# The gate columns of the dense experts: two matmuls per token in the rounded 32-bit format in place of one fp32 matmul

## The chip, the cores and the metric

The kernel runs on one core of a Trainium2 chip. The metric is the device time of one execution in microseconds (us). Before the change three runs gave 3235.85, 3254.53 and 3223.81 us, a median of 3235.85 us.

## What is computed

One encoder layer over 1024 tokens of width 1024: gated attention and convolution, then a retrieval layer over 128 x 128 = 16384 small experts, then a norm. The change lies in the retrieval layer, which in the reference is:

```python
q = (xc @ w_query).reshape(c, PEER_HEADS, 2, PEER_HALF_DIM)
sc = jnp.einsum('chpd,hpnd->chpn', q, sub_keys)
s1, i1 = lax.top_k(sc[:, :, 0], PEER_TOPK)
s2, i2 = lax.top_k(sc[:, :, 1], PEER_TOPK)
cand = (s1[..., :, None] + s2[..., None, :])       # 16 x 16 sums per head
top, pos = lax.top_k(cand, PEER_TOPK)              # 16 experts per head, 8 heads
g = softmax(top)                                    # one gate per chosen expert
a = gelu(einsum('chkd,cd->chk', expert_u[eidx], xc))
out = einsum('chk,chkd->cd', g * a, expert_v[eidx])
```

Each token so has 128 chosen experts (8 heads of 16), each named by two key numbers from 0 to 127 and carrying one gate.

## The kernel before, in words

The tokens are cut into eight tiles of 128. The first five (640 tokens, group B) are served **densely**: every one of the 16384 experts is computed for them by matmul and multiplied by a gate that is zero where the expert was not chosen. The last three (384 tokens, group A) are served by **gathering** the chosen rows of the expert tables with indirect DMAs. Order of the work: queries, keys and values for all tokens; the mixer, output product and expert scores of group B; then the same for group A; then the expert stage, in which the dense products (`passes`, L905) and the gathered rows (`gather_gen`, L739 to L755) run side by side.

The change lies in `weights_gen` (L686). It makes the dense gates of group B while group A's mixer runs. For each of the five tiles, here called a chunk, it waits until the selection has filled `chosen`, transposes the two key numbers and the gate (`ptw`, L703), so that the 128 chosen experts of a token lie on the partitions, and copies the gates to `w` (tile `wtr`, L707). Then 32 steps follow, each for four tokens (`WQ`). In a step VectorE (DVE) compares the key numbers with a row of numbers, which gives the one-hot matrices `ms` (L714); GpSimd (POOL) multiplies the first with the gates, `o1` (L718); ScalarE (ACT) copies the second, `o2` (L720). Both write with another order of the two free dimensions than they read. One step later `finish` (L691) has TensorE (PE) multiply `o2` and `o1` for each of the four tokens (`pw`, L695): over the 128 chosen experts this sums the gates into a 128 x 128 table of key pairs. ACT copies the table to `wbuf` (L696), and after each 32 tokens `wbuf` is written to HBM (`w_d`, L726). The expert stage reads `w_d` back (`wt`, L920) and multiplies it with the experts' outputs (L930). In the profile the tiles `o1` and `o2` are both called `o`.

`ms`, `o1` and `o2` have two buffers each (`WFB = 2`), and so has the PSUM tile `pw`. A buffer of `o1` is free for a later step once PE has done the `pw` matmuls that read it; a buffer of `ms` is free once POOL and ACT have read it.

Elsewhere the kernel already uses the rounded 32-bit format (`F32R`): `put` (L183) writes a rounded copy of a tile on ACT and the rest, tile less copy, on DVE, and `gemm` (L220) and `passes` (L901) make three matmuls of such pairs: high by high, high by low, low by high.

The order of the work is set in two steps. Generators such as `weights_gen` and the selection are advanced by `tick`, which the large products call with an estimate of their time (a step of the gates each 1.6 us of it, `W_STEP`). What is written then goes through a scheduler, which settles the order on each engine's queue before the kernel runs; on the chip each engine works through its own queue in that order.

Of the group A work, `mix` (L524) computes the rows of the output product and their norm, in tiles of a ring called `mixw`, and `repeated_iota` (L111) makes the rows of numbers.

Of the kernel before, what the change touches and what calls it, by code (L numbers as in the profile page):

```python
# [10 lines left out]
F32 = mybir.dt.float32  # L11
BF16 = mybir.dt.bfloat16
F32R = mybir.dt.float32r
# [3 lines left out]
ALU = mybir.AluOpType  # L17
# [3 lines left out]
P = 128  # L21
# [14 lines left out]
NK = 128  # L36
# [15 lines left out]
WQ = 4  # L52
# [5 lines left out]
MIXW = 3  # L58
# [7 lines left out]
def block_kernel(ctx, tc, x, wqkv, wcols, wpr, wo, wq, skT, uv, uT, an_w, fn_w, fin_w, sub_w,  # L66
                 conv_w, lq1, lk1, lq2, lk2, cosT, sinT, out):
    nc = tc.nc
    V, A, PL, PE, SP = nc.vector, nc.scalar, nc.gpsimd, nc.tensor, nc.sync
# [4 lines left out]
    def pool(name, bufs=1, stack=None, **kw):  # L74
        return (stack or left).enter_context(tc.tile_pool(name=name, bufs=bufs, **kw))
# [30 lines left out]
    def rows_bcast(pl, src, n, name, tag=None, bufs=None):  # L106
        t = pl.tile([P, n], F32, name=name, tag=tag or name, bufs=bufs)
        SP.dma_start(out=t, in_=bass.AP(tensor=src.tensor, offset=src.offset, ap=[[0, P], [1, n]]))
        return t

    def repeated_iota(pl, dst, tag="iota"):  # L111
        n = dst.shape[1]
        row = pl.tile([P, n], F32, name="iota", tag=tag, bufs=2)
        PL.iota(row, pattern=[[1, n]], base=0, channel_multiplier=0, allow_small_or_imprecise_dtypes=True)
        V.tensor_copy(out=dst, in_=row.unsqueeze(2).broadcast_to(list(dst.shape)))

# [55 lines left out]
    def norm_rows(src, w_b, dst, junk, tag):  # L172
        ss = tiny.tile([P, 1], F32, name=f"ss_{tag}", tag=f"ss_{tag}")
        A.activation(junk, src, AF.Square, accum_out=ss)
        r = rstd_of(ss, D, 1, tag)
        V.scalar_tensor_tensor(dst, src, r, w_b, op0=ALU.mult, op1=ALU.mult)
# [22 lines left out]
    def transposes(src, dst, t0):  # L199
        for k0 in range(0, KD, 4):  # L200
            if isinstance(dst, tuple):
                to = lambda pt, k0=k0: put(dst, (slice(None), slice(k0, k0 + 4), slice(t0, t0 + P)), pt)
            else:
                to = dst[:, k0:k0 + 4, t0:t0 + P]
            four_transposes(to, [src[:, (k0 + k) * P:(k0 + k + 1) * P] for k in range(4)])
# [8 lines left out]
    def units_k(wp, src, n):  # L214
        u = [unit(wp, src[n, i], 512) for i in range(2)]
        return [tuple(t[:, k % 4, :] for t in u[k // 4]) for k in range(KD)]
# [3 lines left out]
    def gemm(pd, lhs, rhs, us=0.853):  # L220
        n = len(lhs)
        for i in range(n):
            l, r = lhs[i], rhs[i]
            if not isinstance(l, tuple):
                l, r = (l,), (r,)
            c = THREE if len(l) == 2 else ((0, 0),)
            for j, (a, b) in enumerate(c):
                PE.matmul(pd, lhsT=l[a], rhs=r[b], start=i == 0 and j == 0, stop=i == n - 1 and j == len(c) - 1)  # L228
        tick(us * n)

    def kts(op, sl):
        if isinstance(op, tuple):
            return [tuple(t[:, k, sl] for t in op) for k in range(op[0].shape[1])]
        return [op[:, k, sl] for k in range(op.shape[1])]

    def row(wk, name):
        return wk.tile([P, D], F32, name=name, tag="row")
# [286 lines left out]
    def mix(tt0, nt, c0, keep_hn, rings, mT, hnT, outer=None):  # L524
        with ExitStack() as st:
            if outer:
                st = outer
            wk = pool("mixw", nt + MIXW, stack=st)
            fn_b = rows_bcast(pool("mixn", stack=st), fn_w, D, "fn_b")
            xts = []  # L530
            for i in range(nt):
                tt = tt0 + i
                xts.append(row(wk, "xt2"))
                SP.dma_start(out=xts[i], in_=x[tt * P:(tt + 1) * P, :])
            later = []
            for j in range(2):
                w = units_k(rings[j], wo, j)
                for i in range(nt):
                    tt, xt = tt0 + i, xts[i]
                    ph = ps["g"].tile([P, 512], F32, name="ph2", tag="g")  # L540
                    gemm(ph, kts(mT, slice(c0 + i * P, c0 + (i + 1) * P)), w)
                    V.tensor_add(xt[:, j * 512:(j + 1) * 512], ph, xt[:, j * 512:(j + 1) * 512])
                    if j == 1:
                        SP.dma_start(out=h_d[tt * P:(tt + 1) * P, :], in_=xt)
                        hn = row(wk, "hn")
                        norm_rows(xt, fn_b, hn, hn, "h")
                        if keep_hn:
                            SP.dma_start(out=hn_d[tt * P:(tt + 1) * P, :], in_=hn)
                        if later:
                            transposes(*later.pop(0))  # L550
                        later.append((hn, hnT, c0 + i * P))
            if outer:
                return lambda: transposes(*later.pop(0))
            transposes(*later.pop(0))
# [131 lines left out]
    def weights_gen(wf):  # L686
        later = []
        iota_t = wf.tile([P, NK, WQ], BF16, name="iota_t", tag="iota_t", bufs=1)
        repeated_iota(wf, iota_t, "wtr")

        def finish(buf, q, o1, o2):  # L691
            for t in range(0, WQ, 4):
                pw = ps["w"].tile([P, 4, NK], F32, name="pw", tag="g")
                for u in range(4):
                    PE.matmul(pw[:, u, :], lhsT=o2[:, t + u, :], rhs=o1[:, t + u, :], start=True, stop=True)  # L695
                A.copy(out=buf[:, :, q + t:q + t + 4], in_=pw.rearrange("p t i -> p i t"))  # L696

        for c in range(NB):
            while c >= len(chosen):
                yield  # L700
            pt = ps["w"].tile([P, 4, P], F32, name="ptw", tag="g")
            for j, s in enumerate(chosen[c]):
                PE.transpose(out=pt[:, j, :], in_=s, identity=ident)  # L703
            ib = wf.tile([P, 2, P], BF16, name="ib", tag="ib", bufs=2)
            A.copy(out=ib, in_=pt[:, 0:2, :])
            w = wf.tile([P, P], F32, name="wtr", tag="wtr", bufs=2)
            A.copy(out=w, in_=pt[:, 2, :])  # L707
            for b in range(P // WT):
                buf = wf.tile([P, NK, WT], F32, name="wbuf", tag="wbuf", bufs=1)
                for q in range(0, WT, WQ):  # L710
                    ts = slice(b * WT + q, b * WT + q + WQ)
                    sh = [P, NK, WQ]
                    ms = wf.tile([P, 2] + sh[1:], BF16, name="ms", tag="ms")
                    V.tensor_tensor(out=ms, in0=ib[:, :, ts].unsqueeze(2).broadcast_to([P, 2] + sh[1:]),  # L714
                                    in1=iota_t.unsqueeze(1).broadcast_to([P, 2] + sh[1:]), op=ALU.is_equal)
                    o1 = wf.tile([P, WQ, NK], F32, name="o1", tag="o1")
                    o2 = wf.tile([P, WQ, NK], F32, name="o2", tag="o2")
                    PL.tensor_tensor(out=o1.rearrange("p t i -> p i t"), in0=ms[:, 0],  # L718
                                     in1=w[:, ts].unsqueeze(1).broadcast_to(sh), op=ALU.mult)
                    A.copy(out=o2.rearrange("p t i -> p i t"), in_=ms[:, 1])  # L720
                    if later:
                        finish(*later.pop(0))
                    later.append((buf, q, o1, o2))
                    yield
                finish(*later.pop(0))
                A.dma_start(out=w_d[c * (P // WT) + b], in_=buf)  # L726
# [131 lines left out]
    n = NA * P  # L858
# [9 lines left out]
    ms = pa.enter_context(ExitStack())  # L868
# [4 lines left out]
    ps["g"] = pspool("ps_x1", 4, pa)  # L873
    hnT = operand(pool("hnA", stack=pa), [P, KD, n], "hnT")
    mix(NB, NA, 0, True, (wring, wring), mT, hnT)
    with ExitStack() as st:
        sk = pool("sk1", stack=st).tile([P, 2 * PH, NK], F32, name="sk")
# [165 lines left out]
```

## Time and profile before

| what | value |
|---|---|
| median of three runs | 3235.85 us (3223.81 to 3254.53) |
| profiled execution | 3236.47 us |
| its span in the trace | 3234.7 us |
| PE matmul busy | 3017.4 us, 93% |
| PE weight load busy | 2768.1 us, 86% |
| DVE busy | 2647.0 us, 82% |
| ACT busy | 1298.3 us, 40% |
| POOL busy | 954.6 us, 30% |

The span is the time from the first to the last instruction in the trace; some 2 us lie around it. The busy times of PE and of its weight load overlap. Matmuls are pipelined, so the pace of a run of matmuls is read from the distance of their starts, not from the duration of one. A matmul on fp32 operands leaves two records of PE and two of its weight load; a matmul in the rounded format leaves one of each.

### The profile page before, as it was taken

How to read it: one execution, taken by the hardware profiler on the slowest of the kernel's cores; microseconds unless marked ns; L12 is line 12 of the kernel's file. 1: busy time of each engine (PE TensorE's matmuls, PEld its weight loads, DVE VectorE, ACT ScalarE, POOL GpSimd, SP SyncE). 2: the span in 40 equal slices, each digit the busy share in tenths (PEclk: the TensorE clock that was granted, in tenths of full speed). 3: DMA queues.
4: the chain of work that ended last, by engine and by line, in shares of the span. 5: the costliest groups of instructions: out<-in, count | busy, mean ns of one | idle time of the engine just before them, and what ended most of it. 6: DMA issues, size and time to landing. Idle time of an engine off the chain costs nothing.

```text
span 3234.7 us, 46047 instructions
## 1 busy us (share of the span) xinstructions
PE 3017.4 (93%) x17551; PEld 2768.1 (86%) x17551; DVE 2647.0 (82%) x4665; ACT 1298.3 (40%) x2344; POOL 954.6 (30%) x716
## 2 busy tenths in 40 slices
PE   7999999898999889799999999999999999999992
PEld 6799988798888779798989989889888999998891
DVE  4442565478999996798999999999999999998898
ACT  3322464335567757433333333333333333333332
POOL 2310000045444444232223323322333323233333
PEclk9999999999999989899999999999999999999996
DMA  5451232555444374787888888878789899988997
GB/s 177 146 177 66 82 111 92 211 164 202 146 177 182 148 269 161 265 297 274 304 291 293 308 286 315 323 275 316 268 301 339 325 348 338 339 329 317 327 331 288
DMA packets 237550, 801.12 MB, mean 248 GB/s; under 512 B 18832, under 2 KB 123280, under 8 KB 174096
## 3 DMA queue, kind: packets, MB, share of 16 engines
q0 software_dynamic: 64704, 442.53, 37.4%
q1 hardware_dynamic: 152592, 305.30, 27.2%
q10 hardware_dynamic: 20032, 50.34, 4.1%
q8 instruction: 138, 2.26, 0.3%
q14 instruction: 84, 0.69, 0.1%
HBM read 714.74 MB, written 83.36 MB: 247 GB/s over the span
## 4 chain that ended last, share of the span: by engine, by line
PE 36%; DVE 20%; issue 18%; DMA 15%; POOL 7%; ACT 3%; SPq 0%; POOLq 0%; ACTq 0%; DVEq 0%
DMA wt<-w_d 7%; PE z L905 7%; POOL uvt L739 6%; PE pg L228 4%; DMA uvt<-in_uv,idx 4%; PE pq L228 4%; PE pout L905 4%; DVE acc L755 3%; PE ph L228 3%; DVE uvt L746 3%; PE held L905 2%; PE py L228 2%; PE pw L695 2%; DVE hacc L957 2%; PE pv L228 1%
## 5 line engine op out<-in xcount | busy, mean ns | idle before, releaser
L739 POOL DMA_INDIRECT uvt<-in_uv,idx x384 | 552.6, 1439 | 1297.0 <-DVE acc L755 852.8
L905 PE MATMUL z<-actTh,uh 128*128 128x320 f32 x2048 | 636.7, 311 | 2.1 <-ACT pr L929 1.1
L905 PE MATMUL z<-actTh,uhl 128*128 128x320 f32 x2048 | 637.6, 311 | 0.0
L905 PE MATMUL z<-actTl,uh 128*128 128x320 f32 x2048 | 636.1, 311 | 0.0
L746 DVE SCALAR_TENSOR_TENSOR uvt<-uvt,hng 128x1024 f32<-128x1024 f32 x384 | 472.7, 1231 | 48.6 <-DMA uvt<-in_uv,idx 42.9
L755 DVE SCALAR_TENSOR_TENSOR acc<-uvt,wt,acc 128x1024 f32<-128x1024 f32 x381 | 486.4, 1277 | 6.1 <-ACT wt L749 4.8
L905 PEld LDWEIGHTS z<-actTh,uh 128*128 128x128 f32 x2048 | 387.1, 189 | 12.2 <-ACT pr L929 2.1
L905 PEld LDWEIGHTS z<-actTl,uh 128*128 128x128 f32 x2048 | 387.4, 189 | 8.8
L905 PEld LDWEIGHTS z<-actTh,uhl 128*128 128x128 f32 x2048 | 387.9, 189 | 4.0
L905 PE MATMUL pout<-vh,ph 128*128 128x512 f32 x768 | 306.5, 399 | 47.0 <-DVE hacc L957 30.2
L748 ACT ACTIVATE wt<-zt 128x1 f32<-128x1 f32 x384 | 77.5, 202 | 668.4 <-DVE uvt L746 667.5
L905 PE MATMUL pout<-vhl,ph 128*128 128x512 f32 x768 | 302.7, 394 | 0.0
L905 PE MATMUL pout<-vh,phl 128*128 128x512 f32 x768 | 301.9, 393 | 0.6 <-DVE phl L898 0.6
L718 POOL TENSOR_TENSOR o<-ms,wtr 128x512 f32<-128x512 bf16 x160 | 204.7, 1322 | 256.5 <-PE pw L695 127.3
L957 DVE TENSOR_TENSOR hacc<-pout,hacc 128x512 f32<-128x512 f32 x384 | 260.5, 681 | 2.8 <-PE pout L905 2.8
L185 DVE TENSOR_TENSOR wl<-wr,wh 128x2048 fp32r<-128x2048 f32 x66 | 157.2, 2382 | 118.8 <-ACT wh L184 114.7
L896 ACT CAST ph<-pr 128x640 fp32r<-128x640 f32 x128 | 93.3, 729 | 394.2 <-DVE pr L930 394.2
L905 PEld LDWEIGHTS pout<-vh,ph 128*128 128x128 f32 x768 | 145.7, 190 | 78.7 <-DVE hacc L957 39.5
L695 PE MATMUL pw<-o,o 128*128 128x128 f32 x1280 | 172.3, 288 | 39.8 <-POOL o L718 20.2
L184 ACT CAST wh<-wr 128x2048 fp32r<-128x2048 f32 x74 | 141.1, 1909 | 168.8 <-DMA wr<-in_wq 41.5
L695 PEld LDWEIGHTS pw<-o,o 128*128 128x128 f32 x1280 | 164.3, 201 | 47.7 <-POOL o L718 26.9
L905 PE MATMUL held<-vh,ph 128*128 128x512 f32 x512 | 200.6, 392 | 0.7 <-ACT ph L896 0.7
(290 smaller groups left out, 6760.4 us busy)
## 6 DMA issues: line engine op xcount, KB each, us to landing
raw<-in_uT SPq DMA_DIRECT2D x128, 512.0 KB, 6.5
raw<-in_uv SPq DMA_DIRECT2D x128, 512.0 KB, 8.0
w_d<-wbuf ACTq DMA_DIRECT2D x20, 2048.0 KB, 7.0
wt<-w_d SPq DMA_DIRECT2D x32, 1280.0 KB, 16.0
wr<-in_wcols SPq DMA_DIRECT2D x28, 1024.0 KB, 5.1
wr<-in_wq SPq DMA_DIRECT2D x24, 1024.0 KB, 5.2
xt<-in_x SPq DMA_DIRECT2D x16, 512.0 KB, 4.0
q_d<-qt POOLq DMA_DIRECT2D x32, 256.0 KB, 3.5
```

What stands on the lines that cost most here:

```text
L184: A.copy(out=op[0][sl], in_=src)
L185: lo.tensor_sub(op[1][sl], src, op[0][sl].bitcast(F32))
L228: PE.matmul(pd, lhsT=l[a], rhs=r[b], start=i == 0 and j == 0, stop=i == n - 1 and j == len(c) - 1)
L695: PE.matmul(pw[:, u, :], lhsT=o2[:, t + u, :], rhs=o1[:, t + u, :], start=True, stop=True)
L718: PL.tensor_tensor(out=o1.rearrange("p t i -> p i t"), in0=ms[:, 0], in1=w[:, ts].unsqueeze(1).broadcast_to(sh), op=ALU.mult)
L739: PL.indirect_dma_start(out=t[:], out_offset=None, in_=uv, in_offset=bass.IndirectOffsetOnAxis(ap=sels[c][1][:, k:k + 1], axis=0))
L746: V.scalar_tensor_tensor(u, u, 1.0, st[c], op0=ALU.mult, op1=ALU.mult, accum_out=zt)
L748: A.activation(wt, zt, AF.Gelu)
L755: V.scalar_tensor_tensor(st["acc"], v, wt, st["acc"], op0=ALU.mult, op1=ALU.add)
L896: A.copy(out=hi, in_=t)
L905: PE.matmul(ps, lhsT=lhs[k][a], rhs=rhs[k][b], start=first and k == 0 and j == 0, stop=last and k == n - 1 and j == 2)
L957: V.tensor_add(hacc[:, t - NR, ds], ps, hacc[:, t - NR, ds])
```

## The change

The table of a token is made by two matmuls in the rounded format in place of one in fp32. The gate is split in a rounded part (ACT) and a rest (DVE). POOL makes a one-hot matrix for each part, so `o1` doubles in size, and both are summed in PSUM. `o2` holds zeros and ones and is written once, in the rounded format. To make room, the row of numbers and `w` have one buffer in place of two, and `mix` of group A has five tiles in its ring in place of six.

```diff
-    def repeated_iota(pl, dst, tag="iota"):
+    def repeated_iota(pl, dst, tag="iota", bufs=2):
...
-            wk = pool("mixw", nt + MIXW, stack=st)
+            wk = pool("mixw", nt + MIXW - (tt0 > 0), stack=st)
...
-        repeated_iota(wf, iota_t, "wtr")
+        repeated_iota(wf, iota_t, "wtr", 1)
...
                 for u in range(4):
-                    PE.matmul(pw[:, u, :], lhsT=o2[:, t + u, :], rhs=o1[:, t + u, :], start=True, stop=True)
+                    for j in range(2):
+                        PE.matmul(pw[:, u, :], lhsT=o2[:, t + u, :], rhs=o1[:, j, t + u, :],
+                                  start=j == 0, stop=j == 1)
...
-            w = wf.tile([P, P], F32, name="wtr", tag="wtr", bufs=2)
-            A.copy(out=w, in_=pt[:, 2, :])
+            w = wf.tile([P, 2, P], F32R, name="wtr", tag="wtr", bufs=1)
+            A.copy(out=w[:, 0, :], in_=pt[:, 2, :])
+            V.tensor_sub(w[:, 1, :], pt[:, 2, :], w[:, 0, :].bitcast(F32))
...
-                    o1 = wf.tile([P, WQ, NK], F32, name="o1", tag="o1")
-                    o2 = wf.tile([P, WQ, NK], F32, name="o2", tag="o2")
-                    PL.tensor_tensor(out=o1.rearrange("p t i -> p i t"), in0=ms[:, 0],
-                                     in1=w[:, ts].unsqueeze(1).broadcast_to(sh), op=ALU.mult)
+                    o1 = wf.tile([P, 2, WQ, NK], F32R, name="o1", tag="o1")
+                    o2 = wf.tile([P, WQ, NK], F32R, name="o2", tag="o2")
+                    for j in range(2):
+                        PL.tensor_tensor(out=o1[:, j].rearrange("p t i -> p i t"), in0=ms[:, 0],
+                                         in1=w[:, j, ts].bitcast(F32).unsqueeze(1).broadcast_to(sh), op=ALU.mult)
```

## Rows read from the trace of the kernel before

**Rows 1.** Busy us by stretch: start:end, length, PE, PEld, DVE, ACT, POOL, clock, DMA, GB/s
```profile
727.00:858.00 131.00, 117.19 (x748) 115.09 (x747) 118.04 (x358) 77.25 (x101) 64.90 (x41) 0.96 0.49 179
858.00:974.00 116.00, 106.01 (x667) 102.54 (x666) 111.20 (x299) 75.35 (x104) 50.35 (x38) 0.96 0.47 173
974.00:1095.00 121.00, 110.96 (x750) 103.46 (x748) 118.55 (x292) 94.41 (x169) 51.68 (x43) 0.96 0.41 153
1095.00:1214.00 119.00, 96.09 (x568) 86.58 (x566) 111.69 (x273) 74.62 (x102) 55.04 (x42) 0.91 0.67 245
1214.00:1316.00 102.00, 99.58 (x692) 98.63 (x691) 67.27 (x154) 72.58 (x106) 43.29 (x34) 1.00 0.46 165
1316.00:3234.00 1918.00, 1806.58 (x9984) 1636.87 (x9982) 1753.69 (x2642) 632.96 (x1314) 585.59 (x402) 0.98 0.86 310
```

**Rows 2.** Instructions of line L707: ns min/median/max, first and last start, us
```profile
L707 ACT COPY wtr<-ptw x5: 271/280/286, 727.2 to 1214.8; 128x128 f32<-128x128 f32 x5
```

**Rows 3.** Chain of waits from 727 to 1316 us: share of the stretch by line
```profile
by line: PE pq L228 10.9%; PE pw L695 9.6%; issue 9.3%; DVE ms L714 7.5%; PE ph L228 4.7%; PE pg L228 4.4%; DVE wl L185 4.2%; ACT o L720 3.5%; DMA sc<-sc_d 3.3%; DVE tk L590 2.8%; DVE nm L387 2.1%; POOL o L718 1.9%; DVE si L592 1.8%; DMA w_
```

**Rows 4.** Chain of waits from 1200 to 1360 us: start, us, what
```profile
1241.27 1.78 PE pw L695 x16
...
1315.83 10.15 DMA w_d<-wbuf
...
1326.00 20.01 DMA wt<-w_d
```

**Rows 5.** Costliest groups, 727 to 1316 us: count, busy us, mean ns, idle before
```profile
L695 PE MATMUL pw<-o,o 128*128 128x128 f32 x1280 | 172.3, 288 | 39.8 <-POOL o L718 20.2 <-ACT wbuf L696 11.1 <-ACT o L720 8.5
...
L695 PEld LDWEIGHTS pw<-o,o 128*128 128x128 f32 x1280 | 164.3, 201 | 47.7 <-POOL o L718 26.9 <-issue 19.4
...
L718 POOL TENSOR_TENSOR o<-ms,wtr 128x512 f32<-128x512 bf16 x160 | 204.7, 1322 | 256.5 <-PE pw L695 127.3 <-DVE ms L714 107.4 <-DVE sv L591 4.3
```

**Rows 6.** PE in time: first and last of 23 rounded matmuls in a row
```profile
646.11 0.28 PE L228 MATMUL pq<-actTl,wh 128*128 128x256 f32 x1
...
648.72 0.28 PE L228 MATMUL pq<-actTh,wl 128*128 128x256 f32 x1
```

**Rows 7.** Transposes in the rounded format: PE in time; their weight loads
```profile
106.16 0.46 PE L191 MATMUL pt<-ident_r,kst 128*128 128x128 f32 x4
106.46 0.47 PE L228 MATMUL pk<-wh,actTl 128*128 128x512 f32 x1
...
L191 PEld LDWEIGHTS pt<-ident_r,kst x64: 138/140/210, 33.6 to 178.8; 128*128 128x128 f32 x64
```

**Rows 8.** DVE: one-hots (all; 727 to 1214), then splits (727 to 1214; 500 to 720)
```profile
L714 DVE TENSOR_TENSOR ms<-ib,iota_t x160: 654/681/3409, 734.4 to 1311.4; 128x1024 bf16<-128x1024 bf16 x160
...
L714 DVE TENSOR_TENSOR ms<-ib,iota_t 128x1024 bf16<-128x1024 bf16 x128 | 103.9, 822 | 6.5 <-ACT o L720 4.9 <-POOL o L718 1.4
L185 DVE TENSOR_TENSOR wl<-wr,wh 128x2048 fp32r<-128x2048 f32 x24 | 60.8, 2532 | 5.1 <-ACT wh L184 5.0
...
L185 DVE TENSOR_TENSOR wl<-wr,wh 128x2048 fp32r<-128x2048 f32 x12 | 27.5, 2291 | 32.4 <-ACT wh L184 28.4 <-PE pq L228 4.0
```

**Rows 9.** POOL in the last chunk: group from 1214 to 1316; two pairs in time
```profile
L718 POOL TENSOR_TENSOR o<-ms,wtr 128x512 f32<-128x512 bf16 x32 | 39.5, 1296 | 51.8 <-PE pw L695 37.1 <-DVE ms L714 6.4 <-DVE sv L591 4.3
...
1236.69 2.14 POOL L718 TENSOR_TENSOR o<-ms,wtr 128x512 f32<-128x512 bf16 x2 [1.77 <-PE pw L695]
...
1242.25 2.11 POOL L718 TENSOR_TENSOR o<-ms,wtr 128x512 f32<-128x512 bf16 x2 [3.42 <-PE pw L695]
```

**Rows 10.** PE in time: the last four tokens of the last chunk
```profile
1313.58 1.13 PE L695 MATMUL pw<-o,o 128*128 128x128 f32 x8 [0.28 <-POOL o L718]
```

**Rows 11.** Ring `mixw` of group A: first write-out, landing times of `h_d`, third norm
```profile
1174.21 0.33 SPq L544 DMA_DIRECT2D h_d<-xt  x1
...
DMA to landing us min/median/max: 2.6/7.3/11.0
...
1195.39 1.26 DVE L176 SCALAR_TENSOR_TENSOR hn<-xt,r_h,fn_b 128x1024 f32<-128x1024 f32 x1
```

More of the change, by code (lines that the diff above doesn't have):

```diff
@@ L109, in rows_bcast @@
         return t
-    def repeated_iota(pl, dst, tag="iota"):
+    def repeated_iota(pl, dst, tag="iota", bufs=2):
         n = dst.shape[1]
-        row = pl.tile([P, n], F32, name="iota", tag=tag, bufs=2)
+        row = pl.tile([P, n], F32, name="iota", tag=tag, bufs=bufs)
         PL.iota(row, pattern=[[1, n]], base=0, channel_multiplier=0, allow_small_or_imprecise_dtypes=True)
```

## The prediction, made before the result was known

> **What bounds the kernel now.** I read first where the gates are made. The gate copies mark the five chunks: the first at 727.2 us, the last at 1214.8 us [rows 2], and the last store of the gates is issued at 1315.83 us [rows 4]. So the change touches 589 us of the 3234.7, from 727 to 1316 us; the 1918 us after it hold no edited line. Cutting the busy times at the chunks [rows 1] shows two different limits. In the first four chunks, 487 us long, DVE is busy 118.0 + 111.2 + 118.6 + 111.7 = 459.5 us, 94%, and PE 430 us, 88%. In the last chunk PE is busy 99.6 of 102 us and DVE only 67.3. POOL is busy 265 us of the 589, under half.
>
> Next the chain of waits. In the stage it runs over PE, DVE and waits for data in turn [rows 3]: `pw` has 9.6% of it (57 us), DVE's one-hots, splits and selection (`ms`, `wl`, `tk`, `nm`, `si`) 18.4% together (108 us), POOL's `o` only 1.9% (11 us). Behind the stage the chain goes through the last gates themselves: the store of `w_d`, 10.15 us, and the load `wt`, 20.01 us [rows 4]. So when the last gate is ready sets when the dense products can be scaled, and a delay of the last chunk goes to the end in full.
>
> **The change part by part.**
>
> *PE, the matmuls.* Before, 640 tokens leave 1280 records [rows 5]; sixteen of them take 1.78 us on the chain [rows 4], 111 ns each, so 1280 x 0.111 = 142 us of PE, 223 ns a token. After, there are again 1280 records, now each a matmul of its own. The trace of before has no rounded matmul with 128 moving columns. The nearest with an ordinary weight load has 256: 23 of them start from 646.11 to 648.72 us, 22 distances, 119 ns each [rows 6]. From below: transposes in the rounded format, 128 columns, four in 106.46 - 106.16 = 0.30 us, 75 ns each [rows 7]. But a transpose's weight load lasts 140 ns [rows 7] where that of `pw` lasts 201 [rows 5], 61 ns more, so the transposes are no model for a load. I read the 111 ns of the fp32 records as the pace of one weight load after another, and take 115 ns, between 111 and 119: 1280 x 0.115 = 147 us, 5 us more than before, of which the chain's share (57 of 142) makes 2 us. The ends I keep: 75 ns, 46 us less PE; and 223 ns, what a whole fp32 matmul of this shape takes now, if the rounded format gains nothing at this width: 143 us more.
>
> [...]
>
> *POOL.* 160 multiplications become 320 of the same shape: 204.7 us more [rows 5], POOL at about 470 of 589 us, 80%. What hides it: before, POOL idled 256.5 us ahead of these, 127.3 of them waiting for PE to free a buffer and 107.4 for DVE's one-hots [rows 5]. In the last chunk two steps start at 1236.69 and the next two at 1242.25 us, 5.56 us apart, for 2.14 us of work [rows 9]; four multiplications take 4.3 us, or 5.2 at the chunk's mean of 1296 ns [rows 9]. They fit, with under half a microsecond to spare, and the chunk's 51.8 us of idle time fall to some 12. Where POOL is on the chain now, 11 us, the cost doubles: +11 us. In that lies the end, where the last steps come one at a time and PE waits for POOL already [rows 10].
>
> *DVE beside POOL.* A one-hot takes 681 ns in the median but 822 in the mean over the first four chunks, and a split of a weight tile 2532 ns against 2291 in a stretch in which POOL makes no gates [rows 8]. 128 x 0.141 + 24 x 0.24 = 24 us; I take that as time lost to POOL, and a doubling of POOL's gates as up to 24 us more. The bounds are 0 and 24 us. DVE's idle time in the four chunks is 27.5 us [rows 1], part of it waits that will stay; I put 11 us on the chain. A later one-hot holds up what stands behind it on DVE, the selection of the next tile and the evictions PE waits for.
>
> *The rest.* The rest of the gates on DVE: five subtractions of 128 x 128, each no more than a one-hot of eight times the size, under 5 x 0.68 = 3.4 us; I take 1. The single buffer of `w`: ACT's copy for the next chunk waits for POOL's last multiplication, but the chunk's last `wbuf` copy, ahead of it on ACT, waits for that through PE anyhow; nothing, unless the scheduler moves it forward. The ring with five tiles: the third `hn` (written at 1195.39 us) takes the tile whose write-out was issued at 1174.21 us and landed at most 11.0 us later [rows 11]; 10 us to spare, so nothing. ACT writes the same `o2` elements: nothing.
>
> Sum: 2 + 11 + 11 + 1 = 25 us. From the profiled execution's 3236.47 us (its median stands 0.6 us lower, at 3235.85) that gives 3261; I say **3260 us**.
>
> **The rivals.**
>
> *The load does not bound* (chance 0.25). With 75 ns the chain's `pw` shrinks by 57 x 36/111 = 18 us. Against POOL's and DVE's 23 us this ends at about 3241, no change; with those costs hidden as well, at 3218, and only if all 46 us of PE came through, at 3190. For it: the rounded transposes. [...] Against it: the first four chunks are DVE's more than PE's, and the last would then be paced by POOL's 4.3 to 5.2 us a pair, about today's 5.56.
>
> *Rounded matmuls of 128 columns run no faster than fp32* (0.12), slower than before. The price is 143 us of PE, in a stage with 589 - 530 = 59 us of PE idle time [rows 1], so at least 84 us longer: 3320 to 3380. It decides from about 160 ns a matmul, where the extra 63 us no longer fit that idle time. Against it: the transposes' pace.
>
> *POOL becomes the bound* (0.20), slower too. Four multiplications outgrow the 5.56 us of a pair once one takes over 1.39 us; 1322 ns is the stage's mean now [rows 5], with half the collisions. With 1.6 us, 320 make 512 us, and with POOL's other 60 us the stage of 589 us has 17 to spare, which two buffers and queues of fixed order cannot use: I put 60 to 80 us on it, 3295 to 3315. DVE's one-hots then wait for POOL to release `ms`, and PE stands at `pw` with its products queued behind. For it: PE waited 20.2 us for POOL already [rows 5].
>
> **How the numbers follow.** My own case has 0.43 (3235 to 3285), the rivals 0.25, 0.12 and 0.20. One per cent, 32 us, is about what a measurement can tell from no change here, as the three runs lie 31 us apart. Slower by more: both slow rivals, 0.32, and a fifth of my own case, together 0.41. Faster by more needs the fast matmul with POOL's and DVE's costs hidden: 0.12. Within: 0.47. The range runs from 3205, which leaves out the last tenth on the fast side, to 3345, which takes in POOL as the bound and the lower half of the slow matmuls.
>
> **What would show it.** Starts of the `pw` matmuls 111 to 119 ns apart: my price; 75: the first rival; over 160: the second. POOL's gates at about 410 us with 320 instructions, and the time from the first gate copy to the last `w_d` store at about 614 us. If POOL leads what PE and DVE wait for by tens of microseconds, the third rival holds. A mean of `ms` well over 822 ns in the first four chunks would show the collisions. The stretch from the last store to the end should stay near 1918 us; if it moves by over 15 us, the order of the expert stage has changed, which I have not priced. I am wrong above all if DVE's collisions are hidden or the load is.

## The result, and the profile after

Four runs of the changed kernel took 3313.8 to 3320.69 us, median 3318.62; four of the kernel before, on the same chip, 3223.81 to 3254.53, median 3232.65. The ratio on record is 1.0244, 95% interval 1.0210 to 1.0278: 2.4% slower (the two medians alone stand at 1.0266, inside that interval). In the profile the span is 3318.6 us, 83.9 more than before.

First the page's line of busy times (us, share of the span, number of instructions):

```profile
PE 3084.0 (93%) x17551; PEld 2823.6 (85%) x17551; DVE 2704.7 (82%) x4670; ACT 1298.8 (39%) x2340; POOL 1127.9 (34%) x876
```

DVE has five instructions more than before, the five subtractions, and is busy 57.7 us longer. Its idle time went from 587.7 to 3318.6 - 2704.7 = 613.9 us, 26.2 more; the two together are the 83.9.

Next the stage in which the gates are made: the gate copies and the stores of the gates (min/median/max ns, first and last start in us).

```profile
L709 ACT CAST wtr<-ptw x5: 272/273/303, 743.1 to 1331.2; 128x128 fp32r<-128x128 f32 x5
...
L730 ACTq DMA_DIRECT2D w_d<-wbuf x20: 326/327/352, 794.6 to 1450.3; - x20
```

It begins 16 us later than before [rows 2] (`e2` below begins as late, at 744.4 us, and loses 0.3% in all) and lasts 707 us, to 1450.3, where it lasted 589 [rows 2, 4]. What follows it takes 1868 us where it took 1918. The same stretches as in [rows 1], cut at the new chunks (start:end, length, busy us of PE, PEld, DVE, ACT, POOL, granted clock, DMA share, GB/s):

```profile
743.00:906.00 163.00, 140.97 (x816) 136.41 (x814) 152.71 (x416) 79.90 (x106) 104.42 (x74) 0.88 0.39 141
906.00:1054.00 148.00, 125.88 (x734) 117.12 (x732) 133.84 (x320) 89.16 (x136) 92.56 (x73) 0.86 0.40 145
1054.00:1196.00 142.00, 120.99 (x731) 112.39 (x731) 131.30 (x306) 88.79 (x146) 94.22 (x75) 0.88 0.48 170
1196.00:1331.00 135.00, 119.98 (x727) 113.44 (x726) 98.98 (x227) 82.12 (x112) 93.77 (x69) 0.89 0.53 194
1331.00:1450.00 119.00, 79.22 (x370) 72.35 (x369) 113.35 (x326) 60.82 (x85) 87.45 (x70) 0.60 0.35 130
1450.00:3318.00 1868.00, 1807.13 (x9984) 1637.51 (x9984) 1700.24 (x2410) 623.72 (x1304) 548.12 (x399) 0.99 0.87 316
```

PE's work in the last stretch is what it was, 1807 us, but DVE has 53.5 us less to do there [rows 1]: 232 instructions of the selection for group A and of the split of the expert tables now stand in the longer stage, where DVE is busy 103 us more than before. The order on each queue is the scheduler's, so it was settled before the run. The stage's 118 us are therefore not all lost; some 50 come back later. The last chunk is another one than before: PE busy 79 of 119 us instead of 99.6 of 102, DVE 113 of 119 instead of 67, with 326 instructions instead of 154. POOL is busy 472 of 707 us, 67%, and never more than 74% in a chunk.

The costliest groups of 743 to 1451 us that answer to [rows 5, 8] (count, busy us, mean ns, idle time before and its releasers):

```profile
L722 POOL TENSOR_TENSOR o<-ms,wtr 128x512 fp32r<-128x512 bf16 x320 | 406.5, 1346 | 185.1 <-DVE ms L717 107.5 <-PE pw L696 67.2 <-PE pc L228 5.1
L696 PE MATMUL pw<-o,o 128*128 128x128 f32 x1280 | 218.8, 315 | 91.1 <-POOL o L722 52.7 <-ACT o L724 13.6 <-ACT wbuf L698 13.3
L696 PEld LDWEIGHTS pw<-o,o 128*128 128x128 f32 x1280 | 203.1, 230 | 110.0 <-POOL o L722 80.2 <-issue 27.5
...
L717 DVE TENSOR_TENSOR ms<-ib,iota_t 128x1024 bf16<-128x1024 bf16 x160 | 153.2, 962 | 32.4 <-POOL o L722 31.9 <-ACT ib L707 0.5
```

POOL's 320 multiplications take 406.5 us, twice the 204.7 of before; one takes 1346 ns. PE's wait for them rose from 20.2 to 52.7 us, DVE's from 10.1 to 31.9, and a one-hot from 829 ns to 962 [rows 5; the 10.1 and the 829 are from the same view of before]. Over the first four chunks alone the mean of `ms` is 969 ns, where it was 822 [rows 8]: the sign that the prediction named for collisions. PE's busy 218.8 us need not alarm: the starts give the pace (PE in time, us, duration).

```profile
1209.56 1.78 PE L696 MATMUL pw<-o,o 128*128 128x128 f32 x15
1211.18 0.91 PE L228 MATMUL ph<-wh,mTh 128*128 128x512 f32 x3
...
1389.07 3.65 PE L696 MATMUL pw<-o,o 128*128 128x128 f32 x16 [2.69 <-POOL o L722]
```

Fifteen rounded matmuls in 1.62 us, 108 ns each, where the granted clock was 1.00 (1205 to 1225 us; the 0.89 above is the mean of the chunk); sixteen in 3.65 us in a stretch with a granted clock of 0.50 that lasts from 1361 us to the end of the stage while PE has little but these matmuls left.

What POOL does to DVE can be seen in the timeline of the last chunk (start, us, duration):

```profile
1440.07 2.06 POOL L722 TENSOR_TENSOR o<-ms,wtr 128x512 fp32r<-128x512 bf16 x2 [3.02 <-DVE ms L717]
...
1441.16 1.02 DVE L644 TENSOR_TENSOR dv<-tv 128x64 f32<-128x64 f32 x1
...
1445.82 2.06 POOL L722 TENSOR_TENSOR o<-ms,wtr 128x512 fp32r<-128x512 bf16 x2
1445.87 1.07 DVE L649 TENSOR_TENSOR gw<-tv,zz 128x64 f32<-128x64 f32 x1
1446.86 1.07 DVE L635 TENSOR_TENSOR pf<-pf,pj 128x64 bf16<-128x64 bf16 x1
...
1446.94 0.48 PE L696 MATMUL pw<-o,o 128*128 128x128 f32 x1 [3.00 <-POOL o L722]
...
1447.94 1.76 PE L696 MATMUL pw<-o,o 128*128 128x128 f32 x7 [0.52 <-POOL o L722]
```

Two DVE instructions of 64 columns take 1.07 us each, one for each of POOL's two multiplications, and `dv` ends with POOL's pair. `pf` (L635) takes 213 ns in the mean of the kernel before; `gw` and `dv` take 869 and 792 ns there, so those two were long before the change as well. PE can do one matmul after the first multiplication; the other seven start a microsecond later, when the second is done. These are the two candidates: POOL holds up DVE, and POOL's second multiplication lengthens the path from one-hot to matmul.

### The profile page after: what moved, and what is told of

It reads as the page before. It is cut to its first block, busy times and chain, and to the rows that moved or that the text cites. A ratio compares the mean times of both kernels' runs of the same rounds, so it can differ in the third digit from the quotient of the medians.

```text
span 3318.6 us, 46226 instructions
## 1 busy us (share of the span) xinstructions
PE 3084.0 (93%) x17551; PEld 2823.6 (85%) x17551; DVE 2704.7 (82%) x4670; ACT 1298.8 (39%) x2340; POOL 1127.9 (34%) x876
## 4 chain that ended last, share of the span: by engine, by line
issue 21%; PE 10%; POOL 8%; DVE 8%; DMA 8%; ACT 0%; POOLq 0%; DVEq 0%; ACTq 0%
POOL uvt L743 8%; PE z L909 5%; DMA uvt<-in_uv,idx 3%; DMA wt<-w_d 3%; PE pout L909 3%; DVE acc L759 2%; PE held L909 2%; DVE uvt L750 2%; DMA raw<-in_uT 1%; DVE hacc L961 1%; DVE vhl L902 1%; DVE uhl L902 1%; DVE pr L934 0%; DVE phl L902 0%; DVE e L640 0%
## 5 line engine op out<-in xcount | busy, mean ns | idle before, releaser
L743 POOL DMA_INDIRECT uvt<-in_uv,idx x384 | 526.6, 1371 | 1281.1 <-DVE acc L759 1033.6
L722 POOL TENSOR_TENSOR o<-ms,wtr 128x512 fp32r<-128x512 bf16 x320 | 406.5, 1346 | 185.1 <-DVE ms L717 107.5
L909 PE MATMUL pout<-vh,ph 128*128 128x512 f32 x768 | 306.0, 398 | 35.5 <-DVE hacc L961 34.1
L696 PE MATMUL pw<-o,o 128*128 128x128 f32 x1280 | 218.8, 315 | 91.1 <-POOL o L722 52.7
L696 PEld LDWEIGHTS pw<-o,o 128*128 128x128 f32 x1280 | 203.1, 230 | 110.0 <-POOL o L722 80.2
L724 ACT CAST o<-ms 128x512 fp32r<-128x512 bf16 x160 | 178.0, 1121 | 83.9 <-DVE ms L717 71.6
L900 ACT CAST uh<-raw 128x1024 fp32r<-128x1024 f32 x128 | 134.1, 1047 | 175.5 <-DMA raw<-in_uT 88.4
```

Of the source, the lines that this page charges most:

```text
L696: PE.matmul(pw[:, u, :], lhsT=o2[:, t + u, :], rhs=o1[:, j, t + u, :], start=j == 0, stop=j == 1)
L722: PL.tensor_tensor(out=o1[:, j].rearrange("p t i -> p i t"), in0=ms[:, 0], in1=w[:, j, ts].bitcast(F32).unsqueeze(1).broadcast_to(sh), op= ...
L743: PL.indirect_dma_start(out=t[:], out_offset=None, in_=uv, in_offset=bass.IndirectOffsetOnAxis(ap=sels[c][1][:, k:k + 1], axis=0))
L900: A.copy(out=hi, in_=t)
L909: PE.matmul(ps, lhsT=lhs[k][a], rhs=rhs[k][b], start=first and k == 0 and j == 0, stop=last and k == n - 1 and j == 2)
```

## The experiments

All ratios are to the kernel before, run beside on the same chip. "The stage" is the time from the first gate copy to the last store of the gates.

**Which half of the change costs: POOL's second multiplication, or PE's matmuls.** `e1_pool_twice` keeps the fp32 format and one matmul per token, and has POOL multiply into the half of `o1` that PE doesn't read, ahead of the half that it reads: a dummy of the same size. `e2_pe_only` has the two rounded matmuls, both on the rounded part, and one multiplication; its gates count the rounded part twice.

```diff
 e1, against the changed kernel
-                    for j in range(2):
-                        PE.matmul(pw[:, u, :], lhsT=o2[:, t + u, :], rhs=o1[:, j, t + u, :], ...)
+                    PE.matmul(pw[:, u, :], lhsT=o2[:, t + u, :], rhs=o1[:, 0, t + u, :], start=True, stop=True)
...
-                    for j in range(2):
+                    for j in (1, 0):
                         PL.tensor_tensor(out=o1[:, j]...   # o1, o2, w in F32
 e2, against the changed kernel
-                        PE.matmul(pw[:, u, :], lhsT=o2[:, t + u, :], rhs=o1[:, j, t + u, :],
+                        PE.matmul(pw[:, u, :], lhsT=o2[:, t + u, :], rhs=o1[:, 0, t + u, :],
...
-                    for j in range(2):
+                    for j in range(1):
                         PL.tensor_tensor(out=o1[:, j]...
```

> The gate columns in fp32 with one matmul per token as before, but POOL makes two multiplications a step as after (the first writes a half of the tile that nobody reads); the smaller ring, the single buffers and the subtraction are those of after. The stage from the first gate copy to the last store of the gates is 589 us before and 707 after. Theory POOL (the second multiplication, in series with the step, made the stage longer): stage 690 to 710 us, time 3305 to 3325 us. Theory PE (two rounded matmuls a token did): stage 585 to 600 us, time 3225 to 3245 us. Theory order (the rounded matmuls have another price for the scheduler, which ordered the queues worse): as theory PE.

> Two rounded matmuls per token as after, but POOL makes only the product with the rounded gate, and both matmuls read it; the rest of the gates is left out and the rounded part counted twice. Theory POOL: stage 585 to 605 us, time 3225 to 3250 us, starts of the pw matmuls 111 ns apart at the full granted clock as in the kernel after. Theories PE and order: stage 690 to 710 us, time 3305 to 3325 us.

`e1`: 3316.89 us, 1.0237 (1.0217 to 1.0258), the whole loss with the old matmuls; its stage takes 700 us. `e2`: 3249.24 us, 1.0029 (1.0007 to 1.0052), its stage 592 us. The page line of `e1`:

```profile
PE 3069.5 (93%) x17551; PEld 2805.6 (85%) x17551; DVE 2720.0 (82%) x4670; ACT 1296.1 (39%) x2340; POOL 1161.4 (35%) x876
```

its groups of POOL's gates and of `ms`:

```profile
L720 POOL TENSOR_TENSOR o<-ms,wtr 128x512 f32<-128x512 bf16 x320 | 418.1, 1384 | 157.5 <-DVE ms L715 93.3 <-PE pw L695 53.1 <-DVE sf L611 4.3
...
L715 DVE TENSOR_TENSOR ms<-ib,iota_t 128x1024 bf16<-128x1024 bf16 x160 | 159.9, 1006 | 24.6 <-POOL o L720 20.8 <-ACT o L722 2.2 <-ACT ib L705 1.6
```

and the page line of `e2`:

```profile
PE 3041.4 (94%) x17551; PEld 2790.0 (86%) x17551; DVE 2651.9 (82%) x4670; ACT 1299.6 (40%) x2344; POOL 965.7 (30%) x716
```

DVE's extra time comes with the second multiplication (2720.0 us) and goes with it (2651.9; 2647.0 before). The matmuls, the subtraction and the single buffers cost 0.3% together.

**Is there a point at which POOL gets full?** `e5_pool_half` is `e1` with the dummy multiplication on two of the four tokens.

```diff
-                    for j in (1, 0):
-                        PL.tensor_tensor(out=o1[:, j].rearrange("p t i -> p i t"), in0=ms[:, 0], ...)
+                    for j, m in ((1, WQ // 2), (0, WQ)):
+                        PL.tensor_tensor(out=o1[:, j, 0:m].rearrange("p t i -> p i t"), in0=ms[:, 0, :, 0:m], ...)
```

> As e1_pool_twice (fp32, one matmul a token, a second POOL multiplication that nobody reads, ahead of the first), but the second covers two of the four tokens: 128 x 256, about 0.6 us. Theory capacity (POOL has room until its work outgrows the interval between pairs of steps, as the prediction had it): most of the growth of 111 us lies in the second half, stage below 620 us, time below 3260 us. Theory latency (each microsecond more on POOL lies in series with the step, so the stage grows from the first one on): half the growth, stage 635 to 655 us, time 3265 to 3290 us.

3286.34 us, 1.0142 (1.0105 to 1.0180), with 338.4 us of multiplications and a stage of 658 us. In POOL's time this is 134 of the 213 us that `e1` adds, 63%, and the loss is 60% of that of `e1`: in proportion, as far as one point can tell. A free stretch that ends in a knee between `e5` and `e1` is excluded; one that ends earlier is not.

**The path, by the order on POOL.** `e6_pool_behind` does exactly the work of `e1`, but the multiplication that PE waits for comes first.

```diff
-                    for j in (1, 0):
+                    for j in (0, 1):
```

> As e1_pool_twice, but the second multiplication is behind the one that PE reads, so PE need not wait for it; it still takes POOL's time and holds the buffers of ms and o1 longer. Theory latency from one-hot to matmul: the stage falls back by more than half, below 645 us, time below 3275 us. Theory occupancy (POOL's own time and what it holds, ms above all, set the pace): stage 680 to 705 us, time 3300 to 3325 us.

3279.48 us, 1.0118 (1.0079 to 1.0157). The page line:

```profile
PE 3052.6 (93%) x17551; PEld 2795.2 (85%) x17551; DVE 2719.3 (83%) x4670; ACT 1301.6 (40%) x2342; POOL 1144.4 (35%) x876
```

the groups of `pw` in `e1` and then `e6`:

```profile
L695 PE MATMUL pw<-o,o 128*128 128x128 f32 x1280 | 207.3, 316 | 92.6 <-POOL o L720 81.1 <-issue 11.3
L695 PE MATMUL pw<-o,o 128*128 128x128 f32 x1280 | 199.6, 309 | 72.2 <-POOL o L720 49.2 <-ACT wbuf L696 15.4 <-ACT o L722 7.0
```

and the stages of `e1` and then `e6`, in the columns of the table of stretches above:

```profile
745.20:1445.00 699.80, 569.58 (x3371) 531.16 (x3369) 643.40 (x1587) 399.52 (x579) 483.70 (x360) 0.87 0.44 158
740.80:1423.50 682.70, 559.38 (x3370) 524.19 (x3368) 631.40 (x1513) 401.44 (x578) 481.82 (x359) 0.89 0.44 162
```

DVE's busy time in all is that of `e1` to a microsecond, so its collisions stayed; the time fell by 1.2%. PE's wait for POOL fell from 81.1 to 49.2 us. Half of the loss thus goes when the second multiplication moves behind the other. That this is the microsecond between the one-hot and the matmul is the likely reading, but not shown. The stage is 683 us, what was expected of occupancy, while the time lies just above what was expected of latency; of the 38 us between the two profiles 17 lie in the stage, 16 behind it and 4 ahead of it. And the edit changes more than POOL's order: the scheduler settles all queues anew for each kernel, and DVE has the same 4670 instructions here in another order, 1513 of them in the stage where `e1` has 1587. What that other order is worth was not tested.

**Reading or only writing.** `e9_pool_write` puts two fills of the unread half in the place of `e1`'s dummy multiplication. They take about the same time on POOL as one multiplication (two of 528 ns in the median against 1128) and read nothing.

```diff
-                    for j in (1, 0):
-                        PL.tensor_tensor(out=o1[:, j].rearrange("p t i -> p i t"), in0=ms[:, 0], ...)
+                    for _ in range(2):
+                        PL.memset(o1[:, 1], 0.0)
+                    PL.tensor_tensor(out=o1[:, 0].rearrange("p t i -> p i t"), in0=ms[:, 0], ...)
```

> As e1_pool_twice (fp32, one matmul a token), but in place of the second multiplication POOL fills the unread half of the tile twice with zeros: about the same time on POOL (2 x 0.53 us against 1.14), at the same place ahead of the first multiplication, but it reads nothing from SBUF. Theory collisions (the reading multiplication holds up DVE's instructions with two inputs, and DVE bounds the kernel from end to end): DVE busy falls from 2720 to 2645 to 2670 us, time 3235 to 3265 us. Theory series (each microsecond more on POOL lies in series with the step, whatever it does): stage 680 to 700 us, time 3290 to 3320 us.

3249.36 us, 1.0030 (1.0010 to 1.0050). The page line:

```profile
PE 3038.6 (93%) x17551; PEld 2787.3 (86%) x17551; DVE 2658.7 (82%) x4670; ACT 1297.4 (40%) x2342; POOL 1077.2 (33%) x1036
```

and the groups of POOL's gates and of `ms`:

```profile
L721 POOL TENSOR_TENSOR o<-ms,wtr 128x512 f32<-128x512 bf16 x160 | 208.6, 1308 | 58.9 <-DVE ms L715 58.7
L720 POOL MEMSET o<- 128x512 f32 x320 | 168.0, 545 | 126.9 <-PE pw L695 126.2
...
L715 DVE TENSOR_TENSOR ms<-ib,iota_t 128x1024 bf16<-128x1024 bf16 x160 | 138.6, 874 | 34.1 <-POOL o L721 30.5 <-ACT ib L705 3.4
```

DVE's busy time is 61 us below that of `e1` and the loss is gone, down to the 0.3% of `e2`: what the theory of collisions had, and not that of a series. One thing the edit does beside its aim: a fill needs no one-hot. It waits for PE to free the buffer (126.2 us) and not for `ms`. Yet the fills are not off the path. POOL's multiplication waits for its one-hot as follows (us in all, times, longest):

```profile
POOL o L721 <- DVE ms L715: 58.7, 27, 15.2
```

In the other 133 of the 160 steps no such wait is shown. By the starts and ends in the trace a fill runs between the end of the one-hot and its multiplication in 118 steps, 108 us in all; in `e1` a dummy multiplication does so in all 160 steps, 233 us, and in `e6` (one of an earlier step) in 85, 84 us. So `e9` has about as much in that path as `e6`, without the reads, and the step from `e6` to `e9`, 1.0118 to 1.0030, intervals apart, is the nearest thing here to a price of the reads. It is not a clean one, as POOL is busy 67 us less and the queues are ordered anew. And 108 us of fills in the path cost nothing that can be measured, so the path has no fixed price per microsecond. The stage of `e9` still takes 648 us; a longer stage alone loses little, as later work of DVE stands in it (1519 instructions, 1365 in the stage of `e2`).

**A third buffer.** `e4_o1_three` gives the changed kernel three `o1`, and takes the room from group A's convolution (`convw` with one buffer but for `y`), from `ib` and from the ring `mixw`.

```diff
-                    o1 = wf.tile([P, 2, WQ, NK], F32R, name="o1", tag="o1")
+                    o1 = wf.tile([P, 2, WQ, NK], F32R, name="o1", tag="o1", bufs=3)
```

> The kernel after with three buffers of o1 in place of two, paid for by single buffers in the convolution of group A and in ib and one tile less in the ring of mix. If two buffers tie POOL to PE's order and that is what lengthened the stage: stage at most 650 us, time 3255 to 3285 us. If POOL waits for DVE's one-hots rather than for a buffer (107 against 67 us in the kernel after): stage 690 to 710 us, time 3305 to 3330 us.

3340.57 us, 1.0300 (1.0277 to 1.0323). The stage is 45 us shorter than the change's (662 us), POOL's wait for PE falls from 67.2 to 23.5 us, and the stretch after it is 68 us longer (1936 us). DVE is busy 2728.5 us, 24 more. The selection for group A stands behind the stage again here: DVE has 2643 instructions there, as before the change (2642), where the changed kernel has 2410. Which part of the loss is the room taken from elsewhere, and which this order, can't be told: the run is inconclusive on buffers.

**Other ways to make the gates.** `e3_hi_only` is the change without the rest of the gates: one rounded matmul and one multiplication.

```diff
-                    for j in range(2):
-                        PE.matmul(pw[:, u, :], lhsT=o2[:, t + u, :], rhs=o1[:, j, t + u, :], ...)
+                    PE.matmul(pw[:, u, :], lhsT=o2[:, t + u, :], rhs=o1[:, 0, t + u, :], start=True, stop=True)
...
-                    for j in range(2):
+                    for j in range(1):
```

> One rounded matmul per token and one POOL multiplication a step: the rest of the gates is left out. Theory POOL: PE loses 640 records of 111 ns, 71 us, of which the chain's share before (57 of 142) would make 28 us: time 3205 to 3235 us, stage 560 to 590. Theory PE: between before and after at the least, since a rounded matmul is then dear: 3240 to 3280 us. If the first four chunks are DVE's, the gain is in the last chunk alone: 3220 to 3235.

3227.14 us, 0.9953 (0.9932 to 0.9974). PE's work in `pw` is halved (640 records), some 70 us at 111 ns, and 0.5% comes out: PE then waits for ACT's `wbuf` 34.1 us, for POOL 29.3 and for `o2` 26.9. The stage is not shorter than before (603 us, 560 to 590 expected). So PE's time in `pw` is not what the stage is mainly short of.

`e7_direct_fp32` drops the one-hot of the first key on DVE: POOL makes `o1` from the key numbers in one instruction per token (compare, then multiply by the gate), DVE writes `o2` itself. `e8_direct_hi` is the same in the rounded format with one matmul, without the rest of the gates.

```diff
 e7, against the kernel before
-                    PL.tensor_tensor(out=o1.rearrange("p t i -> p i t"), in0=ms[:, 0], ...)
-                    A.copy(out=o2.rearrange("p t i -> p i t"), in_=ms[:, 1])
+                    V.tensor_tensor(out=o2, in0=ib..., in1=iota_b..., op=ALU.is_equal)
+                    for u in range(WQ):
+                        PL.tensor_scalar(o1[:, u, :], iota_t, i1[:, t:t + 1], w[:, t:t + 1], op0=ALU.is_equal, op1=ALU.mult)
 e8, against e7
-                    o1 = wf.tile([P, WQ, NK], F32, name="o1", tag="o1", bufs=3)
+                    o1 = wf.tile([P, WQ, NK], F32R, name="o1", tag="o1", bufs=3)   # o2 too
```

> The kernel before (fp32, one matmul a token, ring of six), but without the tile ms: POOL writes o1 from the row of numbers with four operations of 128 x 128 (equal to the key number, times the gate), which wait for no one-hot of DVE, DVE writes o2 directly at half the size of ms, and ACT's copy of 179 us goes; o1 and o2 have three buffers. If POOL's waits for DVE and DVE's one-hots set the pace of the first four chunks: stage 540 to 580 us, time 3190 to 3225 us. If PE and the selection do: stage 575 to 590, time 3220 to 3240 us. If POOL's four small operations cost over 2.3 us a step together, as much as two multiplications now: stage over 650, time over 3280 us.

> As e7_direct_fp32, but o1 and o2 in the rounded format and so one weight load and one matmul a token: the rest of the gates is left out, as in e3_hi_only. PE has 71 us less than in e7. If PE is a bound of the stage then: 20 to 40 us below e7, time 3170 to 3205 us. If DVE bounds it: within 15 us of e7.

`e7`: 3317.87 us, 1.0227 (1.0188 to 1.0265); `e8`: 3290.55, 1.0147 (1.0114 to 1.0181). Of what was expected of `e7` the last came, POOL's four operations taking over 2.3 us a step; `e8` is 27 us faster, but far above its expected times. POOL's gates in `e7`:

```profile
L722 POOL TENSOR_SCALAR o<-iota_t,i,wtr 128x128 f32<-128x128 f32 x640 | 638.4, 1009 | 16.2 <-ACT wtr L711 12.8 <-PE pw L697 3.2
```

Here POOL is the bound: busy 705.6 of the stage's 731.5 us. DVE is busy less than before (2618.9 us) and it doesn't help. This is what the prediction's third rival looks like when it holds; in the change POOL is 67% busy.

`e10_bf16_parts` splits the gate in two bf16 parts, POOL making the one and ACT the other; `e11_half_on_act` leaves the format and gives ACT two of each four tokens of `o1`; `e12_half_on_act_hi` is `e11` in the rounded format with one matmul, without the rest of the gates.

```diff
 e10, against the kernel before
+                    o1 = wf.tile([P, 2, WQ, NK], BF16, name="o1", tag="o1", bufs=3)
+                    PL.tensor_tensor(out=o1[:, 0].rearrange("p t i -> p i t"), in0=ms[:, 0], ...)
+                    for u in range(WQ):
+                        A.activation(o1[:, 1, u, :], ms[:, 0, :, u], AF.Copy, scale=wl[:, t:t + 1])
 e11, against the kernel before
+                    PL.tensor_tensor(out=o1[:, 0:m].rearrange("p t i -> p i t"), in0=ms[:, 0, :, 0:m], ...)   # m = 2
+                    for u in range(m, WQ):
+                        A.activation(o1[:, u, :], ms[:, 0, :, u], AF.Copy, scale=w[:, t:t + 1])
 e12, against e11
+                    o1 = wf.tile([P, WQ, NK], F32R, name="o1", tag="o1")   # o2 too
```

> The kernel before, with the gate in two bf16 parts: POOL multiplies the one-hot with the high part once a step as before, ACT makes the low part by four scaled copies of 128 x 128 in place of its copy of o2, and PE makes two bf16 matmuls per token that read the second one-hot directly. POOL and DVE have the work of before. If a weight load of bf16 costs PE what the others do, 111 ns: PE as before, time 3225 to 3250 us. If it is faster, 55 to 85 ns: PE loses 33 to 70 us, as e3_hi_only time 3215 to 3235 us. If ACT's four copies take over 0.45 us each it lengthens the stage: over 3260 us.

> The kernel before in fp32, but POOL makes o1 for two of the four tokens of a step only (128 x 256, about 0.63 us); ACT makes the other two by scaled copies of 128 x 128 (about 0.4 us each). POOL's reading time for the gates falls from 205 to about 105 us, ACT gets some 128 us. Theory collisions, by the slope of the runs so far (DVE busy 2647 at 205 us of POOL's gates, 2705 at 407, 2754 at 442): DVE busy 2615 to 2630 us, time 3205 to 3230 us. Theory series (what counts is POOL's time in the step): the same sign, but only as far as POOL is on the chain, 11 us of it: 3230 to 3240. If ACT with 128 us more becomes the bound: 3245 to 3270.

> As e11_half_on_act, with o1 and o2 in the rounded format and one matmul per token; the rest of the gates is left out, as in e3_hi_only. PE has 71 us less. Theory collisions: DVE busy 2615 to 2635 us, time 3195 to 3225 us, up to 15 us below e11. If ACT is the bound: as e11 within 5 us.

`e10`: 3339.49 us, 1.0327 (1.0300 to 1.0354), the largest ratio of all, though PE's matmuls got shorter (`pw` keeps PE busy 118.6 us, 249 ns a record, where it was 172.3 and 288). None of its three expectations covers this: ACT's copies took 404 ns, under the 0.45 us set. POOL's group in it:

```profile
L721 POOL TENSOR_TENSOR o<-ms,wtr 128x512 bf16<-128x512 bf16 x160 | 441.8, 2874 | 177.4 <-DVE ms L718 155.5 <-DVE rz L395 6.5 <-issue 3.8
```

One multiplication takes 2874 ns in the mean where it took 1322; the edit gives it a bf16 output and a bf16 gate, and which of the two does it was not tested. So POOL is in these multiplications for about as long as in the change (441.8 us, 406.5 there) with half the instructions, and DVE's busy time grows by 107 us, to 2753.8. Again POOL's time in multiplications and DVE's busy time go up together.

`e11`: 3255.21 us, 1.0044 (1.0020 to 1.0068). POOL's gates fall to 128.7 us and DVE's busy time to 2615.6, as the collisions would have it, but no time is won. The groups of `pw` and `ms` say why:

```profile
L695 PE MATMUL pw<-o,o 128*128 128x128 f32 x1280 | 183.3, 293 | 61.9 <-ACT o L724 38.3 <-POOL o L719 9.8 <-ACT wbuf L696 7.1
...
L714 DVE TENSOR_TENSOR ms<-ib,iota_t 128x1024 bf16<-128x1024 bf16 x160 | 118.9, 749 | 51.4 <-ACT o L724 38.1 <-ACT ib L705 7.6 <-POOL o L719 4.9
```

ACT's two scaled copies (409 ns each) now stand before its copy of `o2`, and PE and DVE wait for that. It looks like the path once more, with another engine in it, though nothing here isolates it; the time is what was expected should ACT become the bound. `e12`: 3222.43 us, 0.9938 (0.9915 to 0.9961). It and `e3` are faster than both kernels, but both leave out the rest of the gates, so their gates are coarser than the kernel's before; no version with the whole gates came out faster than before.

## Why the prediction was wrong

The forecast was 3260 us, within 1% of no change; the kernel became 2.4% slower, 3318.62 us. That is above its likeliest case (3235 to 3285) and inside the range, but by luck: the slow end of the range stood for a POOL without room and for slow matmuls, and neither came. By its steps:

*The matmuls: right.* 108 ns by the starts, most of them 111 ns apart, where 111 to 119 was forecast; `e2` prices them and all the rest at 0.3%, some 10 us, against the 2 and 1 us set down. The first two rivals fall with this: neither 75 ns nor 160.

*POOL's own time: right.* 406.5 us against 409 forecast.

*The failed step: "They fit", and "the cost doubles: +11 us".* The sum gave POOL's second multiplication 22 us, 11 on POOL's chain and 11 for DVE beside it. `e1`, which has this multiplication with the old matmuls, loses 77 us, and `e2`, without it, some 10: about 67 us are its price. On POOL's side it was priced by two things: whether four of them fit in the 5.56 us of a pair, and POOL's share of the chain before. Both ask whether POOL has room. It had: 67% busy, 1346 ns, below the 1.39 us that the third rival named as its point. But a matmul waits for its own step's one-hot and multiplications, in order, and room on POOL does not shorten that. Moving the second multiplication behind the one that PE waits for takes back 39 us at the same DVE busy time (`e6`, 1.0237 to 1.0118), where the sum had 11 for POOL's chain. A chain share tells what POOL costs at its present length; it didn't bound what a longer step costs.

*The second mis-sized term: DVE beside POOL, +11 us, bounds 0 and 24.* DVE's busy time grew by 57.7 us, 22.7 of it in `ms`; in `e1` it grew by 73. The forecast took only `ms` and the weight splits from the rows, and the rest is spread over many instructions, some up and some down: `e` (L649) went from 3.9 to 12.6 us, but is at 15.3 in `e2`, which has one multiplication, and `dv` went from 12.7 to 6.7. The best price in time is the step from `e6` to `e9`, 1.0118 to 1.0030, 29 us. DVE is busy 2720.0 us beside multiplications (`e1`) and 2658.7 beside fills (`e9`), and the `gw` and `pf` of 1.07 us above are each as long as a multiplication beside it. By the starts and ends in the trace of the change's stage, the 77 one-hots that start while POOL makes gates take 1215 ns in the mean, the other 83 take 726; the copy `sf` (L611), with one input, takes 962 ns beside the gates (6 times) and 219 otherwise (5), while MAX8 of the selection (`sv`, L591) takes 291 and 288. Why some are held up and others not is not shown.

What is shown is that the second multiplication makes the loss (`e1`, `e2`), that half of it goes when that multiplication is moved behind the other (`e6`), and that fills in its place lose no more than `e2` (`e9`). How the 77 us of `e1` divide is not shown. Read one after the other, the runs give 39 us for the place, 29 for the reads and some 10 that `e2` has as well, the first two within some 14 us each by the intervals. Against taking this for a division stand four things. The 108 us of fills in the path of `e9` cost nothing. DVE's busy time alone could cover the loss of `e1` (its span is 81 us longer than before, with DVE busy 73 us more), though not the 38 us by which the span of `e6` is shorter at the same busy time. Each kernel has its queues ordered anew, a rival that no run holds fixed. And the granted clock at the end of the stage was not isolated: in its last three stretches of some 30 us it was 0.50 throughout in the change and 0.56, 0.50 and 0.56 in `e1`, but 0.94, 0.61 and 0.56 in `e6` and 0.90, 0.71 and 0.69 in `e9`. The change has the same loss as `e1` (1.0244) and the same signs, but was not itself taken apart.

*The rivals.* The time lies between the third's 3295 to 3315 and the second's 3320 to 3380. One of the third's signs came (PE and DVE wait for POOL, 52.7 and 31.9 us), but its mechanism, POOL out of room, is not it: `e5` shows no knee near the full addition, and `e7` shows what a full POOL looks like.

*The stretch after the stage* was to stay near 1918 us, and a delay of the last chunk was to go to the end in full; the stretch is 50 us shorter, so neither held. I had not thought of the scheduler putting later work of DVE into a longer stage. A stage's length is not its price: that of `e9` is 57 us longer than that of `e2`, at the same time in all.

## What to carry to other kernels

Idle time of an engine didn't make work on it free here: POOL was 67% busy in the stage, and its second multiplication cost about 67 us (`e1` less `e2`). Ask how long the path from producer to consumer gets per step, and whether the added instruction lengthens another engine's (a one-hot took 1215 ns beside POOL's gates and 726 otherwise); here 60% of the loss was there at 63% of the addition (`e5`). A dummy copy of the suspected instruction shows whether it is the cause. Put once ahead of and once behind the one that is waited for, and once as a mere write, it helps to tell path and reads apart; but where a scheduler orders the queues anew for each kernel, compare their order too before dividing the loss.

## What the runs showed of the hardware

- A POOL multiplication of 128 x 512 from bf16 with a permuted output takes 1128 ns (`e9`) to 1145 ns (`e3`) in the median with an fp32 or rounded output and an fp32 or rounded gate, but 2712 ns with both in bf16 (`e10`).
- On POOL, comparing and multiplying 128 x 128 with per-partition scalars takes 792 ns in the median, and DVE's busy time did not grow beside 640 of them (`e7`, 2618.9 us; its one-hots are half the size, so the run doesn't isolate this); a fill of 128 x 512 takes 528 ns (`e9`).
- Pairs of weight load and matmul at 128 columns start 111 ns apart in the rounded format (the changed kernel, from 1209.62 us, at a granted clock of 1.00). A weight load of `pw` lasts 192 ns in the median there and 114 in bf16 (`e10`).
- PE's granted clock fell to 0.50 in the last 89 us of the change's stage, where PE was busy some 17 of each 30 us, and was back at 0.99 in the expert stage.
